# A block inverse that joins four 32-row blocks per product instead of two, in a two-block transformer kernel on one Trainium2 core

## The chip, the core and the metric

The kernel runs on one core of one Trainium2 chip. The engines named below are TensorE (PE, with PEld for its weight loads), VectorE (DVE), ScalarE (ACT), GpSimd (POOL) and SyncE (SP), which here only issues transfers, in the order of its own queue. The metric is the device time of one execution in microseconds (us); lower is better.

## The reference, cut to what matters

Two blocks run one after the other over 1024 tokens of width 1024. The first is the one that matters: a projection `z = h @ w_in`, two branches that read it, their gated sum, and a mixture of experts. One branch is latent attention (`mla_branch`). The other is a recurrence of 8 heads of 64 channels in two directions:

```
    def step(state, inp):
        r_t, w_t, k_t, v_t, a_t, b_t = inp
        sa = jnp.einsum('bhvk,bhk->bhv', state, a_t)
        state = (state * w_t[:, :, None, :] + sa[..., None] * b_t[:, :, None, :]
                 + v_t[..., None] * k_t[:, :, None, :])
        return state, jnp.einsum('bhvk,bhk->bhv', state, r_t)
...
    w_logit = w0.astype(f32) + jnp.einsum('bsdr,drc->bsdc', jnp.tanh(wd), w_up.astype(f32))
...
    a = jax.nn.sigmoid(a0.astype(f32) + jnp.einsum('bsdr,drc->bsdc', ad, a_up.astype(f32)))
```

The second block (windowed attention, a gated linear recurrence, two more mixtures of experts) is not touched.

## The kernel before, in words

The first stage, `branches`, holds everything the change touches. `phase_a` computes z^T in 37 column tiles (`z_tile`: 48 products of 128x512 each) and, between tiles, starts the recurrence. Four head pairs (two heads on 128 partitions) go through four steps:

- `prep(p, d, g)`, for each direction d and each half g of the tokens (so four times per pair): two low-rank products (L579, with the operand `lora_up`) give the decay and the a gate; then mostly VectorE work, two sets of 64-token Gram products (`gram`, L551), and transfers to scratch memory. One result is L, a strictly triangular 64x64 matrix for each chunk of 64 tokens.
- `inverse(p)`: (I - L)^-1 of all 64 matrices of a pair. First the 32x32 diagonal blocks by substitution on VectorE, one block per partition (L653, L655). The result goes to scratch memory E (L656, L658) and comes back as tiles `xn` and `xt`. Then, for each of four units (g, d), the products that fill the off-diagonal block: eight products of 128x128 by 32 columns with L (tile `bd`, L671), a copy to a block diagonal tile (L674 on VectorE, L672 on ScalarE), eight more (L676), a copy on GpSimd and an addition on VectorE (L678, L679), and the transfer to `rw` (`put`, L489). The units share two pairs of tiles and one tile for L, so a unit's loads wait for an earlier unit's products.
- `rwkv_chain(p)`: 16 chunks one after the other, each four sets of small products (L732) with copies between.
- `finish(p, g)`: norm, bonus and gate.

`pair(j)` runs prep four times for pair j, with the inverse and the chain of pair j - 1 behind the first. Latent attention (`mla`) comes last in the program; its inputs z are loaded (L792, L794) once the tiles of `phase_a` are free, then come keys and values (L827, L838), and scores, transposes and values (`S`, L889, L904). After both, `branch_out` takes the results (the products `br`).

The program is written in that order, but a scheduler of the framework, with its own estimates of durations, lays down the order of each engine's instructions. At run time every engine, and SP's queue, follows its order strictly. A pool's buffer that is taken again makes its first writer wait for its last reader.

A float32 product appears in the profile as two records, so eight products are 16 records.

Of the kernel before, what the change touches and what calls it, by code (L numbers as in the profile page):

```python
# [7 lines left out]
F32 = mybir.dt.float32  # L8
# [13 lines left out]

ALPHA = float(np.float32(4.0 ** 0.25))
# [4 lines left out]
# ---------------------------------------------------------------- host layout  # L28

def _cols(w, idx):  # L30
    """[K, M] -> [len(idx)//128, 128, (K//128)*128]: tile, k-partition, (k-block, column)."""
    K = w.shape[0]
    t = w[:, idx].reshape(K // 128, 128, len(idx) // 128, 128)
    return np.ascontiguousarray(t.transpose(2, 1, 0, 3).reshape(len(idx) // 128, 128, K))


def _fvec(v):
    """[n*128] -> [128, n]: feature on the partition."""
    return v.reshape(-1, 128).T


def _chunks(w):
    """[..., K, N] -> [..., N/512 * K/512, 128, 2048]: chunks of 4 k-blocks by 512 columns, k fastest."""
    K, N = w.shape[-2:]
    n = w.ndim - 2
    w = w.reshape(*w.shape[:-2], K // 512, 4, 128, N // 512, 512)
    o = list(range(n)) + [n + x for x in (3, 0, 2, 1, 4)]
    return np.ascontiguousarray(w.transpose(o)).reshape(*w.shape[:n], -1, 128, 2048)


def _constants():
    """Constants of the branches, and those of the whole program."""
# [37 lines left out]
def _vectors(i):  # L90
# [9 lines left out]
    perm = np.concatenate([np.arange(1536, 1920), *[  # L100
# [13 lines left out]
def arrays(i):  # L114
# [8 lines left out]
    order = list(range(1536, 1920))  # L123
# [27 lines left out]
    a["a_up"] = np.ascontiguousarray(i["a_up"][0].reshape(128, 512))  # L151
# [39 lines left out]
# ---------------------------------------------------------------- device program  # L191

class Prog:
# [3 lines left out]
    def consts(self, pool, temp):  # L197
        """pool: for the whole program; temp: for the branches."""
# [17 lines left out]
    def keep(self, keep, dram):  # L216
        """Scratch memory, and the small tiles that several phases use."""
# [37 lines left out]
    def slots(self, table, n, base):  # L255
        """What marks the rows in table [128, 8, n, 6]: the row of its block plus base, the block and zero."""
# [5 lines left out]
    def thirds(self, table, x):  # L262
        """x in three bfloat16 parts that add up to it exactly, to table[..., 3:6]; x is overwritten."""
# [7 lines left out]
    def iota8(self, pool):  # L271
        """The slots (from 1), each eight times."""
# [4 lines left out]
    def onehot(self, out, iota8, pm):  # L277
        """out [128, 128, 8]: 1 at the slot pm (from 1) of each row and row block, 0 elsewhere."""
        return self.nc.vector.tensor_tensor(out, iota8, pm[:, None, :].to_broadcast([128, 128, 8]), op=OP.is_equal)

    def mm3(self, ps, lh, ll, rh, rl, first, last):
        """One K block of a float32 product from operands split into float32r parts."""
# [5 lines left out]
    def order(self, later, first):  # L288
        """`later` is issued behind `first` on their engine: one accumulation at a time in a bank."""
# [3 lines left out]
    def rsqrt(self, pool, out, v, n):  # L293
        """out = v ** -0.5 by Newton steps; out, v: [128, n]."""
# [16 lines left out]
    def rsqrt1(self, pool, out, v):  # L311
        """The same for one column where ScalarE has its square root at hand."""
# [9 lines left out]
def s1(P, hpool, wpool, psum):  # L322
    """Reads x, normalises it and leaves its transpose, split, in hT (hi, lo)."""
# [18 lines left out]
def z_tile(P, spool, psum, hT, m, use):  # L342
    """z^T rows of column tile m of w_in; use(s, ps): the PSUM tile of the tokens s."""
# [15 lines left out]
def phase_a(P, zpool, spool, psum, hT, after=lambda j: None):  # L359
    """z^T = (h @ w_in)^T tile by tile; what later phases need goes to scratch memory."""  # L360
# [81 lines left out]
class Rwkv:  # L442
    """The RWKV branch: a head pair (two heads on 128 partitions) and half of the tokens at a time."""
# [13 lines left out]
    def own(self, dram, pool, psw):  # L457
        """Memory for prep alone."""
        self.pp, self.psw, self.bd, self.n = pool, psw, [], 0
        self.inv = [tuple(pool.tile([128, NH, CH], F32, name=f"x{n}{i}", bufs=1) for n in "nt") for i in range(2)]  # L460
        for a in self.inv:
            for t in a:
                self.P.nc.gpsimd.memset(t, 0.0)
        self.L = [dram.tile([4, 128, NH, CH], F32, name=f"rL{i}") for i in range(2)]
        self.E = [dram.tile([128, 2, 32, 32], F32, name=f"rE{i}") for i in range(2)]
        for b in range(4):
# [9 lines left out]
    def t(self, name, tag="t"):  # L476
        n = {"t": 9, "u": 2, "l": 2}[tag]
# [14 lines left out]
    def stats(self, src, scale, u=None):  # L492
        """[128 (h, ch), 512] -> sums over ch per (token, head): [128 t, 8 = (block, h)] times scale."""
# [7 lines left out]
    def spread(self, st, u=None):  # L501
        """[128 t, 8 = (block, h)] -> [128 (h, ch), 512] in PSUM."""
# [8 lines left out]
    def keys(self, p, g):  # L511
        """Normalised kk of head pair p, negated, to scratch memory."""
# [12 lines left out]
    def flip(self, p, d, g, m, x):  # L525
        """x [128 (h, ch), 512 tokens], transposed per head, to part m of the scratch memory."""
# [10 lines left out]
    def diag(self, i, f):  # L537
        """Block diagonal buffer i, written by f(destination, rows) for each head."""
# [6 lines left out]
    def gram(self, lb, AR, da, mask, dr):  # L545
        """lb^T [A | R] of every chunk (partition: the index of lb), under causal masks."""
# [14 lines left out]
    def prep(self, p, d, g):  # L561
        """Chunks 8 g to 8 g + 7 of head pair p in direction d: all that needs no running state, to memory."""
# [5 lines left out]
        ds = slice(64 * d, 64 * d + 64)  # L568
# [7 lines left out]
        for dst, x, act, b in ((sg, 0, P.twd, self.hb[:, n * d + p:n * d + p + 1]),  # L576
                               (ta, 1, P.ad, self.hb[:, n * (2 + d) + p:n * (2 + d) + p + 1])):
            pm = self.ps(0)
            nc.tensor.matmul(pm, up[ds, x], act[ds, ts], start=True, stop=True)  # L579
            nc.scalar.activation(rv(dst), pm, AF.Tanh, bias=b, scale=0.5)  # L580
# [51 lines left out]
    def inverse(self, p):  # L632
        """(I - L)^-1 of every chunk of head pair p: 32 x 32 diagonal blocks by substitution, one block per
        partition (half, direction, h, block, chunk), then the products that join two blocks."""
# [24 lines left out]
        for u in units:  # L659
            self.n += 1  # L660
            Xn, XT = self.inv[self.n % 2]
            LB = self.bd[2]
            for h in range(2):
                s = slice(64 * h, 64 * h + 64)
                nc.sync.dma_start(LB[s, :, s], L[u, s])
            for x, t in ((0, Xn), (1, XT)):
                for h, b in part:
                    nc.sync.dma_start(t[rows(h, b), :, 32 * b:32 * b + 32], E[at(u, h, b), x].rearrange("c i j -> i c j"))
            ps = self.ps(0).rearrange("p (x c t) -> p x c t", x=2, t=32)
            for c in range(NH):  # L670
                nc.tensor.matmul(ps[:, 0, c], LB[:, c], Xn[:, c, 0:32], start=True, stop=True)  # L671
            for h, copy in ((0, nc.vector.tensor_copy), (1, lambda o, i: nc.scalar.activation(o, i, AF.Copy))):  # L672
                s = slice(64 * h, 64 * h + 64)
                copy(self.bd[3][s, :, 64 * h:64 * h + 32], ps[s, 0])  # L674
            for c in range(NH):
                nc.tensor.matmul(ps[:, 1, c], self.bd[3][:, c], XT[:, c, 32:64], start=True, stop=True)  # L676
            out = self.t3("rXT", "u")
            nc.gpsimd.tensor_copy(out[:, :, 0:32], XT[:, :, 0:32])  # L678
            nc.vector.tensor_add(out[:, :, 32:64], ps[:, 1], XT[:, :, 32:64])  # L679
            self.put(p, u % 2, u // 2, 8, out)  # L680

    def finish(self, p, g, u=None):
        """Group norm, bonus and gate of head pair p; half of o_rwkv^T of the pair."""
# [33 lines left out]
def rwkv_chain(P, pool, psum, p):  # L717
    """The running states of head pair p in both directions over the chunks; leaves y^T in scratch memory."""
# [5 lines left out]
    def mm(ps, terms):  # L724
        # one accumulation group per bank: only its first product clears the bank
# [1309 lines left out]
```

## Time and profile before

| What | Value |
|---|---|
| Median of 3 runs | 4299.33 us (4295.06 to 4307.67) |
| Span of the profiled execution | 4303.5 us |
| TensorE busy over the span | 3854.9 us (90%) |
| VectorE busy | 2887.8 us (67%) |
| ScalarE busy | 2145.3 us (50%) |
| GpSimd busy | 418.9 us (10%) |
| Mean granted TensorE clock | 0.930 of full speed |

The runs' times are of the whole execution, and the profiled span lies inside their spread, 4.2 us above their median. Busy time counts an instruction from its start to its modelled end; the granted clock has two levels, 1.2 and 2.4 GHz, and a mean between 0.5 and 1 tells how a stretch was divided between them.

### The profile page before, as it was taken

To read this page: it belongs to the slowest core of one execution; us is meant where nothing else is said; L and a number is where in the kernel's file an instruction comes from. 1 tells how busy PE (TensorE), PEld (TensorE's weight loads), DVE (VectorE), ACT (ScalarE), POOL (GpSimd) and SP (SyncE) were. 2 spreads that over 40 slices of the span, in tenths; PEclk is the share of its full clock that TensorE was granted. 3 is DMA by queue.
4 is the path that set the end of the run, shared out by engine and by line. 5 is a ranking of instruction groups with operands and counts; after the bars stand their busy time and mean duration, and the time that the engine had idled before them with its cause. 6 is when DMAs were issued, how large, how long until landed. Compare 5 with 4: busy or idle time off the path is not lost. (4 is left out here: it accounts for less than half of the span.)

```text
span 4303.5 us, 57981 instructions
## 1 busy us (share of the span) xinstructions
PE 3854.9 (90%) x22154; PEld 3100.3 (72%) x22154; DVE 2887.8 (67%) x4690; ACT 2145.3 (50%) x2829; POOL 418.9 (10%) x328
## 2 busy tenths in 40 slices
PE   7999988898998897999799969999969986999994
PEld 6877766776876676665679857787748875788773
DVE  4556375858557546654446758888876776788887
ACT  4322223333243224555335536777756852677774
POOL 0000000000010003333000001111010000111101
PEclk9999988988899898999899979999979997999997
DMA  3455665453435557997332359999941155899994
GB/s 106 140 169 148 182 196 161 120 153 92 150 107 173 212 193 269 317 304 227 120 132 82 131 205 338 370 376 384 373 158 69 69 202 207 304 359 377 384 373 168
DMA packets 362342, 925.00 MB, mean 215 GB/s; under 512 B 147600, under 2 KB 205712, under 8 KB 290128
## 3 DMA queue, kind: packets, MB, share of 16 engines
q1 hardware_dynamic: 343632, 870.93, 56.4%
q0 software_dynamic: 18432, 50.36, 4.7%
q8 instruction: 175, 2.87, 0.3%
q14 instruction: 103, 0.84, 0.1%
HBM read 770.68 MB, written 167.25 MB: 218 GB/s over the span
## 5 line engine op out<-in xcount | busy, mean ns | idle before, releaser
L253 DVE TENSOR_TENSOR wlo<-wraw,whi 128x2048 fp32r<-128x2048 f32 x498 | 1134.2, 2289 | 307.1 <-ACT whi L253 303.8
L253 ACT ACTIVATE whi<-wraw 128x2048 fp32r<-128x2048 f32 x498 | 955.0, 1919 | 378.3 <-PE g L286 254.0
L285 PE MATMUL g<-wlo,xth 128*128 128x512 f32 x1280 | 510.0, 398 | 6.7 <-DVE wlo L253 6.7
L284 PE MATMUL g<-whi,xth 128*128 128x512 f32 x1280 | 513.7, 402 | 2.3 <-ACT xth L253 1.6
L286 PE MATMUL g<-whi,xtl 128*128 128x512 f32 x1280 | 508.4, 397 | 7.7 <-DVE xtl L253 7.3
L286 PEld LDWEIGHTS g<-whi,xtl 128*128 128x128 f32 x1280 | 243.5, 190 | 63.7 <-DVE xtl L253 12.7
L285 PEld LDWEIGHTS g<-wlo,xth 128*128 128x128 f32 x1280 | 244.0, 191 | 61.4 <-DVE wlo L253 9.1
L284 PEld LDWEIGHTS g<-whi,xth 128*128 128x128 f32 x1280 | 244.4, 191 | 57.3 <-ACT xth L253 3.9
L284 PE MATMUL z<-hT_hi,w_hi 128*128 128x512 f32 x592 | 243.0, 411 | 9.7 <-ACT w_hi L253 6.7
L1635 POOL DMA_INDIRECT e_xg<-xm,e_ix x32 | 75.5, 2359 | 1719.5 <-DVE e_ix L1633 956.6
L285 PE MATMUL z<-hT_lo,w_hi 128*128 128x512 f32 x592 | 242.0, 409 | 0.0
L286 PE MATMUL z<-hT_hi,w_lo 128*128 128x512 f32 x592 | 241.0, 408 | 0.0
L285 PE MATMUL g<-wlo,e_hh 128*128 128x512 f32 x512 | 202.4, 398 | 15.5 <-DVE wlo L253 15.5
L284 PE MATMUL g<-whi,e_hh 128*128 128x512 f32 x512 | 204.3, 400 | 8.2 <-ACT e_hh L253 8.0
L286 PE MATMUL g<-whi,e_hl 128*128 128x512 f32 x512 | 196.5, 391 | 0.2
L904 PE MATMUL po<-V,pts 128*128 128x64 f32 x1024 | 142.5, 285 | 6.3 <-DVE tab L856 4.9
L284 PEld LDWEIGHTS z<-hT_hi,w_hi 128*128 128x128 f32 x592 | 115.2, 195 | 41.5 <-ACT w_hi L253 7.4
L904 PEld LDWEIGHTS po<-V,pts 128*128 128x128 f32 x1024 | 135.4, 204 | 12.1 <-DVE tab L856 5.2
L755 POOL TENSOR_SCALAR SW<-S,wc 128x64 f32<-128x64 f32 x120 | 65.5, 563 | 785.0 <-DVE S L773 701.3
L285 PEld LDWEIGHTS z<-hT_lo,w_hi 128*128 128x128 f32 x592 | 115.0, 194 | 30.4 <-issue 4.5
L286 PEld LDWEIGHTS z<-hT_hi,w_lo 128*128 128x128 f32 x592 | 114.4, 193 | 30.0 <-issue 3.8
L1235 PE MATMUL g<-wraw,m_hT 128*128 128x512 f32 x256 | 120.3, 610 | 13.1 <-ACT m_y L1236 8.1
(531 smaller groups left out, 8308.7 us busy)
## 6 DMA issues: line engine op xcount, KB each, us to landing
wraw<-in_w_gu SPq DMA_DIRECT2D x256, 1024.0 KB
wraw<-in_w_dn SPq DMA_DIRECT2D x128, 1024.0 KB
wraw<-in_w SPq DMA_DIRECT2D x96, 1024.0 KB
rwt<-rw SPq DMA_DIRECT2D x32, 1152.0 KB
w_raw<-in_w_in SPq DMA_DIRECT2D x37, 512.0 KB
rw<-flip SPq DMA_DIRECT2D x96, 128.0 KB
rw<-rAR SPq DMA_DIRECT2D x16, 512.0 KB
gt<-z_out SPq DMA_DIRECT2D x16, 512.0 KB
```

The costliest lines, as they stand in the source:

```text
L253: return self.nc.scalar.activation(hi, src, AF.Copy), self.nc.vector.tensor_sub(lo, src, hi.bitcast(F32))
L284: t.matmul(ps, lh, rh, start=first, stop=False)
L285: t.matmul(ps, lh, rl, start=False, stop=False)
L286: t.matmul(ps, ll, rh, start=False, stop=last)
L755: nc.gpsimd.tensor_scalar(SW[:, d], S[:, d], P.wc[:, c, 4 * d + p:4 * d + p + 1], None, op0=OP.mult)
L904: i = nc.tensor.matmul(po[:, q], pt[:, k], V[:, 4 * q + k, 64 * par:64 * par + 64], start=(k == 0), stop=(k == 3))
L1235: nc.tensor.matmul(ps, ht[:, k], w[:, k, n], start=(k == 0), stop=(k == 1))
L1635: nc.gpsimd.indirect_dma_start(out=xg, out_offset=None, in_=self.x, in_offset=bass.IndirectOffsetOnAxis(ap=ix[:, :1], axis=0))
```

## The change

Two things change in the stage `branches`. First, the inverse: the four 32-row blocks of one half of the tokens (two directions, two heads) stand on the four quarters of the 128 partitions, so that one product with a tile of four diagonal 32x32 blocks serves both directions. The loop runs over the two halves g instead of the four units. All loads of a pair are asked for ahead of the products, into tiles that the halves don't share, and the copies out of PSUM are of 32 rows, half of them on VectorE and half on ScalarE; the last ones go straight into the tile that is put to memory. Second, the weights and columns of the low-rank part are permuted so that the two products of one prep read different halves of the 128 rows, and both products are written ahead of both activations. To make room, the scratch of the software-made transfers (those of GpSimd) is halved from the framework's default of 16384 bytes.

```
+LORA = np.r_[1536:1664, 1728:1792, 1664:1728, 1792:1920]
...
-    a["a_up"] = np.ascontiguousarray(i["a_up"][0].reshape(128, 512))
+    a["a_up"] = np.ascontiguousarray(i["a_up"][0][::-1].reshape(128, 512))
...
-        self.inv = [tuple(pool.tile([128, NH, CH], F32, name=f"x{n}{i}", bufs=1) for n in "nt") for i in range(2)]
+        self.inv = [pool.tile([128, NH, CH], F32, name=f"xt{i}", bufs=1) for i in range(4)]
...
-        for b in range(4):
+        for b in range(5):
             t = pool.tile([128, NH, 128], F32, name=f"bd{b}", bufs=1)
...
-        ds = slice(64 * d, 64 * d + 64)
+        rows = [slice(64 * x, 64 * x + 64) for x in (d, 1 - d)]
...
-        for dst, x, act, b in ((sg, 0, P.twd, self.hb[:, n * d + p:n * d + p + 1]),
-                               (ta, 1, P.ad, self.hb[:, n * (2 + d) + p:n * (2 + d) + p + 1])):
-            pm = self.ps(0)
-            nc.tensor.matmul(pm, up[ds, x], act[ds, ts], start=True, stop=True)
-            nc.scalar.activation(rv(dst), pm, AF.Tanh, bias=b, scale=0.5)
+        pm = [self.ps(0) for x in range(2)]
+        for x, act in enumerate((P.twd, P.ad)):
+            nc.tensor.matmul(pm[x], up[rows[x], x], act[rows[x], ts], start=True, stop=True)
+        for x, dst in enumerate((sg, ta)):
+            o = n * (2 * x + d) + p
+            nc.scalar.activation(rv(dst), pm[x], AF.Tanh, bias=self.hb[:, o:o + 1], scale=0.5)
...
-        for u in units:
-            self.n += 1
-            Xn, XT = self.inv[self.n % 2]
-            LB = self.bd[2]
-            for h in range(2):
-                s = slice(64 * h, 64 * h + 64)
-                nc.sync.dma_start(LB[s, :, s], L[u, s])
-            for x, t in ((0, Xn), (1, XT)):
+        X1, X2 = (pool.tile([128, 2 * NH, 32], F32, name=x, bufs=1) for x in ("rX1", "rX2"))
+        quad = [(d, h, slice(64 * d + 32 * h, 64 * d + 32 * h + 32)) for d in range(2) for h in range(2)]
+        cs = [slice(NH * g, NH * g + NH) for g in range(2)]
+        for g in range(2):
+            for d, h, q in quad:
+                u = 2 * g + d
+                nc.sync.dma_start(self.bd[2 + g][q, :, q], L[u, 64 * h:64 * h + 32, :, 32:64])
+                nc.sync.dma_start(X1[q, cs[g]], E[at(u, h, 0), 0].rearrange("c i j -> i c j"))
+                nc.sync.dma_start(X2[q, cs[g]], E[at(u, h, 1), 1].rearrange("c i j -> i c j"))
+            for d in range(2):
                 for h, b in part:
-                    nc.sync.dma_start(t[rows(h, b), :, 32 * b:32 * b + 32], E[at(u, h, b), x].rearrange("c i j -> i c j"))
+                    nc.sync.dma_start(self.inv[2 * g + d][rows(h, b), :, 32 * b:32 * b + 32],
+                                      E[at(2 * g + d, h, b), 1].rearrange("c i j -> i c j"))
+        copies = (nc.vector.tensor_copy, lambda o, i: nc.scalar.activation(o, i, AF.Copy))
+        for g in range(2):
             ps = self.ps(0).rearrange("p (x c t) -> p x c t", x=2, t=32)
             for c in range(NH):
-                nc.tensor.matmul(ps[:, 0, c], LB[:, c], Xn[:, c, 0:32], start=True, stop=True)
-            for h, copy in ((0, nc.vector.tensor_copy), (1, lambda o, i: nc.scalar.activation(o, i, AF.Copy))):
-                s = slice(64 * h, 64 * h + 64)
-                copy(self.bd[3][s, :, 64 * h:64 * h + 32], ps[s, 0])
+                nc.tensor.matmul(ps[:, 0, c], self.bd[2 + g][:, c], X1[:, NH * g + c], start=True, stop=True)
+            for d, h, q in quad:
+                copies[h](self.bd[4][q, :, q], ps[q, 0])
             for c in range(NH):
-                nc.tensor.matmul(ps[:, 1, c], self.bd[3][:, c], XT[:, c, 32:64], start=True, stop=True)
-            out = self.t3("rXT", "u")
-            nc.gpsimd.tensor_copy(out[:, :, 0:32], XT[:, :, 0:32])
-            nc.vector.tensor_add(out[:, :, 32:64], ps[:, 1], XT[:, :, 32:64])
-            self.put(p, u % 2, u // 2, 8, out)
+                nc.tensor.matmul(ps[:, 1, c], self.bd[4][:, c], X2[:, NH * g + c], start=True, stop=True)
+            for d, h, q in quad:
+                copies[h](self.inv[2 * g + d][64 * h:64 * h + 32, :, 32:64], ps[q, 1])
+            for d in range(2):
+                self.put(p, d, g, 8, self.inv[2 * g + d])
...
-    nc = bacc.Bacc("TRN2", target_bir_lowering=False, num_devices=1)
+    nc = bacc.Bacc("TRN2", target_bir_lowering=False, num_devices=1, dynamic_dma_scratch_size=8192)
```

The scheduler lays down new orders for the stage. On TensorE, the inverse of the second head pair begins like this before the change; the products of one unit are `xn` with `bd` and, some rows on, `xt` with `bd` (each row x8), and latent attention's keys and values (`pj`) stand between.

```order
L671 MATMUL pw<-xn_189,bd_203 128x32 x8
L732 MATMUL pc<-p_2718,rwt 64x64 x4
L827 MATMUL pj<-zk,wk 128x512 x2
...
L838 MATMUL pj<-wv,zk 128x128
L676 MATMUL pw<-xt_190,bd_205 128x32 x8
L838 MATMUL pj<-wv,zk 128x128 x2
L732 MATMUL pc<-p_2768,rwt 64x64 x4
L671 MATMUL pw<-xn_187,bd_203 128x32 x8
```

At the same place after the change, the whole inverse is four such rows (`rX` with `bd`), and the next prep's two low-rank products stand between them:

```order
L680 MATMUL pw<-rX_3921,bd_203 128x32 x8
L740 MATMUL pc<-S,rwt 64x64 x4
L740 MATMUL pc<-rwt 64x64 x4
L740 MATMUL pc<-p_2684,rwt 64x64 x4
L684 MATMUL pw<-rX_3922,bd_207 128x32 x8
...
L680 MATMUL pw<-rX_3921,bd_205 128x32 x8
L580 MATMUL pw<-twd,lora_up 128x512
...
L684 MATMUL pw<-rX_3922,bd_207 128x32 x8
L580 MATMUL pw<-ad,lora_up 128x512
```

The eight groups have become four, attention's keys have moved behind them, and the two low-rank products have three rows between them (two of the chain and the last group). In all 16 preps of the changed order there are rows between the two (2 to 22); in the order before they are neighbours in one prep of 16.

In SP's queue, after the last tile of `phase_a`, attention's inputs stood ahead of the second pair's inverse; its store of E comes as `rE` further down:

```order
L485 DMA v<-zr_102 128x512
L792 DMA zk<-zm_109 128x1024
L792 DMA zk<-zm_110 128x1024
L794 DMA zq<-zm_106 128x1024
L593 DMA kd_140<-t_3749 128x512
L794 DMA zq<-zm_107 128x1024
L794 DMA zq<-zm_108 128x1024
```

After the change the store of E stands behind `v`, ahead of `kd`, and attention's inputs come behind the inverse's loads and the first two of its four puts:

```order
L674 DMA xt_189<-rE_198 32x8x32 x4
L674 DMA xt_190<-rE_198 32x8x32 x4
L490 DMA rw_129<-xt_187 128x4x128
L490 DMA rw_129<-xt_188 128x4x128
L649 DMA rLd<-rL_195 8x32x32 x4
L669 DMA bd_203<-rL_195 32x8x32 x2
L800 DMA zk<-zm_109 128x1024
L800 DMA zk<-zm_110 128x1024
L802 DMA zq<-zm_106 128x1024
```

So the loads of `zk` and `zq` have moved past the puts, which wait for products.

## Rows read from the trace of the kernel before

**Rows 1.** Windows: busy us (instructions) by engine, granted clock, DMA share, GB/s.

```profile
core 0: us, PE busy (x) PEld busy (x) DVE busy (x) ACT busy (x) POOL busy (x), PEclk, DMA share, GB/s
600.00:640.00 40.00, 25.35 (x261) 20.53 (x256) 29.66 (x55) 11.42 (x28) 6.73 (x9) 0.79 0.85 261
640.00:690.00 50.00, 42.12 (x252) 34.63 (x252) 13.21 (x28) 10.75 (x24) 3.39 (x7) 0.55 0.43 111
690.00:850.00 160.00, 140.18 (x1280) 113.49 (x1279) 137.43 (x337) 66.18 (x164) 9.78 (x18) 0.93 0.51 147
850.00:905.00 55.00, 47.83 (x368) 40.68 (x366) 16.83 (x39) 12.11 (x31) 4.35 (x10) 0.73 0.46 114
905.00:1080.00 175.00, 155.06 (x1377) 124.06 (x1378) 136.73 (x328) 66.88 (x167) 12.35 (x20) 0.89 0.45 131
1080.00:1135.00 55.00, 53.43 (x376) 46.61 (x373) 15.39 (x46) 10.16 (x27) 3.30 (x8) 0.66 0.46 121
1135.00:1360.00 225.00, 221.90 (x2585) 179.28 (x2583) 145.09 (x415) 96.04 (x265) 22.19 (x49) 0.99 0.37 124
1360.00:1430.00 70.00, 46.39 (x273) 31.74 (x273) 43.29 (x94) 19.24 (x30) 2.01 (x4) 0.77 0.68 238
```

**Rows 2.** Timeline of PE, end of the stage: start, us, line, product, idle before.

```profile
1364.28 0.66 PE L943 MATMUL pj<-cst,O 128*128 128x128 f32 x4 [0.69 <-ACT ot L945]
...
1377.61 0.64 PE L732 MATMUL pc<-rwt,U 64*64 64x64 f32 x8
...
1392.00 1.41 PE L284 MATMUL br<-oh,whi 128*128 128x512 f32 x1
```

**Rows 3.** Groups by line: busy us, mean ns of one, idle before and its causes.

```profile
L671 PE MATMUL pw<-xn,bd 128*128 128x32 f32 x256 | 44.6, 333 | 10.0 <-DMA bd<-rL 8.4 <-DMA xt<-rE 1.6
L676 PE MATMUL pw<-xt,bd 128*128 128x32 f32 x256 | 40.8, 322 | 8.7 <-ACT bd L672 6.3 <-DMA xt<-rE 2.4
L579 PE MATMUL pw<-twd,lora_up 64*128 64x512 f32 x32 | 20.8, 734 | 0.0
L579 PE MATMUL pw<-ad,lora_up 64*128 64x512 f32 x32 | 18.8, 669 | 0.9 <-DVE nkk L522 0.9
```

**Rows 4.** Timeline of PE, three groups of the third inverse's products.

```profile
864.11 1.97 PE L676 MATMUL pw<-xt,bd 128*128 128x32 f32 x16
...
880.25 1.03 PE L671 MATMUL pw<-xn,bd 128*128 128x32 f32 x4 [6.86 <-DMA bd<-rL]
...
889.05 3.62 PE L676 MATMUL pw<-xt,bd 128*128 128x32 f32 x16
```

**Rows 5.** Timeline of SP's queue during the second inverse: start, us of issuing, transfers.

```profile
602.95 0.90 SPq L792 DMA_DIRECT2D zk<-zm  x2
...
605.54 0.32 SPq L593 DMA_DIRECT2D kd<-t  x1
...
619.33 0.32 SPq L658 DMA_DIRECT2D rE<-rLd  x1
...
639.46 1.93 SPq L668 DMA_DIRECT2D xt<-rE  x4
...
663.01 0.38 SPq L489 DMA_DIRECT2D rw<-rXT  x1
...
684.13 0.38 SPq L489 DMA_DIRECT2D rw<-rXT  x1
685.64 0.33 SPq L572 DMA_DIRECT2D lora_up<-in_w_up  x1
```

**Rows 6.** Timeline of PE, end of the projection and attention's first keys.

```profile
593.46 0.40 PE L286 MATMUL z<-hT_hi,w_lo 128*128 128x512 f32 x1
...
622.86 1.98 PE L827 MATMUL pj<-zk,wk 128*128 128x512 f32 x4 [0.27 <-ACT ot L803]
```

**Rows 7.** Groups by line: the copies between the products, 300 to 1140 us.

```profile
L674 DVE COPY bd<-pw 64x256 f32<-64x256 f32 x16 | 6.7, 416 | 33.6 <-PE pw L671 33.6
L672 ACT ACTIVATE bd<-pw 64x256 f32<-64x256 f32 x16 | 6.0, 378 | 48.1 <-DVE bd L674 48.1
```

**Rows 8.** The page's costliest groups: a software-made transfer.

```profile
L1635 POOL DMA_INDIRECT e_xg<-xm,e_ix x32 | 75.5, 2359 | 1719.5 <-DVE e_ix L1633 956.6 <-PE tr L1057 724.5 <-DVE e_oh L279 25.1
```

More of the change, by code (lines that the diff above doesn't have):

```diff
@@ L98, in add @@
         cols.append(a)
-    perm = np.concatenate([np.arange(1536, 1920), *[
+    perm = np.concatenate([LORA, *[
         np.concatenate([np.arange(128 * p, 128 * p + 128) + 512 * s for s in range(3)]) for p in range(4)]])
@@ L122, in arrays @@
     a["x"] = np.ascontiguousarray(i["x"].reshape(8, 128, D))
-    order = list(range(1536, 1920))
+    order = list(LORA)
     for p in range(4):
@@ L457, in own @@
     def own(self, dram, pool, psw):
-        self.pp, self.psw, self.bd, self.n = pool, psw, [], 0
-        self.inv = [tuple(pool.tile([128, NH, CH], F32, name=f"x{n}{i}", bufs=1) for n in "nt") for i in range(2)]
-        for a in self.inv:
-            for t in a:
-                self.P.nc.gpsimd.memset(t, 0.0)
+        self.pp, self.psw, self.bd = pool, psw, []
+        self.inv = [pool.tile([128, NH, CH], F32, name=f"xt{i}", bufs=1) for i in range(4)]
+        for t in self.inv:
+            self.P.nc.gpsimd.memset(t, 0.0)
         self.L = [dram.tile([4, 128, NH, CH], F32, name=f"rL{i}") for i in range(2)]
         self.E = [dram.tile([128, 2, 32, 32], F32, name=f"rE{i}") for i in range(2)]
-        for b in range(4):
+        for b in range(5):
             t = pool.tile([128, NH, 128], F32, name=f"bd{b}", bufs=1)
@@ L476, in t @@
     def t(self, name, tag="t"):
-        n = {"t": 9, "u": 2, "l": 2}[tag]
+        n = {"t": 9, "l": 2}[tag]
         return (self.big if tag == "t" else self.pp).tile([128, HT], F32, name=name, tag=tag, bufs=n)
```

## The prediction, made before the changed kernel ran

> **What bounds the kernel now.** I first looked in the page's forty slices for the place of the changed lines: they lie in the first third of the span. The chain of waits reaches back from the end only into the expert stages, so it says nothing here; the stage has to be read from windows. Those show a rhythm [rows 1]. In three long stretches VectorE is full (137.43 of 160 us, then 136.73 of 175): preps and substitutions. Between them lie the joins of the inverses (640 to 690, 850 to 905, 1080 to 1135), where VectorE has almost nothing to do (13 to 17 us) and TensorE's granted clock is 0.55 to 0.73. From 1135 to 1360 TensorE is busy 221.90 of 225 us at a clock of 0.99. The end of the stage shows what decides: attention's last products are at 1364, the last chain's at 1378, `branch_out` starts at 1392 [rows 2]. So attention and the recurrence end together and TensorE is full in the last 225 us: what it is spared earlier should arrive as time, since the work that fills it is only moved forward.
>
> The joins are long because they wait: from the second store of E at 619.33 to the last put at 684.13 the second inverse takes 65 us, and the next prep's weights (`lora_up`, 685.64) stand behind that put in SP's queue [rows 5]. VectorE therefore starts its next full stretch only then.
>
> **The change part by part.**
>
> *Half of the products.* 512 records of L671 and L676 are busy 44.6 + 40.8 = 85.4 us [rows 3]. Eight groups of 16 records per pair become four of the same shape, so 42.7 us go. The price of a group is 1.97 us at the high clock and 3.62 at the low one [rows 4]: 16 groups fewer are worth 31.5 us if all ran at 2.4 GHz and 57.9 if all at 1.2. I take 42.7, the mix that the trace shows.
>
> *Waits at these products.* TensorE sat idle 10.0 + 8.7 = 18.7 us in front of them, for `bd` and `xt` loads that a shared tile held back and for the copy between the two sets [rows 3]. The loads now come ahead; the copy stays. Bounds 0 and -18.7; I take half, -9.4.
>
> *The clock in the joins.* After the 6.86 us wait at 880 the next groups run at the low level (3.62 us against 1.97) [rows 4]. The three joins hold 42.12 + 47.83 + 53.43 = 143.4 us of TensorE work at clocks of 0.55, 0.73 and 0.66 [rows 1]; about three quarters of the 85.4 are products of the inverse, which leaves some 79 us of other work at about 0.65. At the 0.93 of the stretch in between that would be 55 us, so the bounds are 0 and -24. The shorter joins still have copies and puts to wait for: I take a third, -8.
>
> *The copies.* Per pair VectorE has eight small instructions before and eight after, ScalarE eight instead of four, GpSimd four fewer; ScalarE is idle most of the stage (10 to 12 us busy in each join [rows 1]), so that is where the extra ones hide. What stands on the path is the row of copies between two sets: now 0.42 + 0.38 us, one after the other (L672 waited 48.1 us for L674 in all) [rows 7]. Four 32-row copies have as many elements per partition, so I price them alike: at most 1.6 us in place of 0.8, twice per half instead of once per unit plus an addition. That is about 1.5 us more per pair if nothing overlaps, 6 in all, 0 if the two engines run side by side; I take +3.
>
> *The loads* are 40 per pair before and after, at about 0.48 us of issue each (1.93 for four) [rows 5], so SP's issue time stays. The transfers are no larger.
>
> *Attention's inputs move.* This is the one thing in the new order that speaks against the change. Before, the loads of `zk` were issued at 602.95 [rows 5] and the first keys came at 622.86, after the projection's last product at 593.46 [rows 6]. Now they stand behind 32 loads and two puts of the second inverse. The store of E now precedes the `kd` store, which was at 605.54 [rows 5], and everything is a little earlier because the first inverse gives back some 8 us; say E is stored at 600. Then 32 loads (15.4 us), about ten other transfers (6 us) and six small loads put `zk` at 625 or so, some 20 us later. In 600 to 640 TensorE was busy 25.35 of 40 us [rows 1] even with attention's first products in it; I count half of the 20 us as new idle time, +9 to +10: I take +9. Bounds: 0 if the chain and the prep fill it, +20 if nothing does. What is queued behind the waiting puts is attention alone; the next prep's weights follow only three places behind its last load and come far earlier than before.
>
> *The low-rank products.* Both are written ahead of both activations, on different row halves. They are busy 20.8 + 18.8 = 39.6 us [rows 3]. TensorE's queue keeps rows of 128x512, 64x64 or 128x128 products between the two in every prep of the new order, so neither has its partner beside it: 0. The bounds are 0 and -19.8. Against that: the Trainium skill, TensorEngine Tiling, section Tiling Modes (Key Properties), says that different tiles of the array can load and multiply in parallel. By that rule two neighbouring half-row products would take the time of one, and the sum would be 19.8 us lower; no run here shows such a pair yet, and the order gives the rule nothing to act on.
>
> *The halved scratch* concerns GpSimd's transfers, all of them in the expert stages. GpSimd sat idle 1719.5 us in front of the 32 loads of L1635 alone [rows 8], so waiting there is covered: 0. Without that cover each of them would be late by what it waits, and I have no row for that.
>
> Sum: -42.7 - 9.4 - 8 + 3 + 9 = -48.1 us, from 4303.5 to 4255.4. The profiled span is 4.2 us above the median of the runs, 4299.33; against that median the same sum gives 4251.
>
> **The rivals.**
>
> *A. The freed time turns into waits (small gain).* VectorE's two full stretches stay as they are, and if the recurrence, not TensorE, is what the end waits for, or attention's late start costs its full +20, only part of 42.7 arrives. For it: 86% busy VectorE from 690 to 850. Against it: TensorE at 221.90 of 225 at the end. Price: 31.5 us of products less 20 is -11.5, to about -25 with a few waits gone: 4274 to 4288.
>
> *B. The joins' waits and clock come back whole.* -42.7 - 18.7 - 24 = -85.4: 4214. For it: two rounds instead of four, and no load between them. Against it: copies, puts and SP's order remain.
>
> *C. The low-rank halves overlap after all*, with each other or with neighbouring half-row products of the chain: -48 - 19.8 = -68: 4231. Against it: the order.
>
> *D. Slower: attention waits for the second inverse.* The place is SP's queue at the two puts ahead of `zk`. If the second put went out as late as before (663.01 [rows 5]), attention's inputs would come about 65 us after 602.95; with half to all of that idle on TensorE, +33 to +65 replaces the +9, and the total is -24 to +8. It turns slower if the put comes later than that by 10 us or more, for instance at 680 with nothing to fill TensorE: +82 - 57 = +25, 4324.
>
> *E. The halved scratch holds GpSimd's transfers back*, or the new order in the stage cancels the gain in some other place: within 13 us of before, 4299.
>
> **How the numbers follow.** A measurement of this kernel can tell about 0.3%, 13 us. Chances: my forecast 0.62, A 0.15, B 0.09, C 0.06, D 0.04, E 0.04. The predicted time is 4251. The forecast's own terms, each at its bounds, run from about -70 to -30: 4229 to 4269. For 8 in 10 the range reaches into A and B: 4212 to 4286. Faster by over 0.3%: forecast, B, C and most of A, 0.87. Within: the rest of A, half of E and a little of D, 0.08. Slower: 0.05.
>
> **What would show it right or wrong.** In the changed profile: the two lines of the inverse's products with 128 records each (L680, L684), 40 to 45 us together; the low-rank products about as busy as before, 38 to 41 us. From the second inverse's store of E to its last put about 30 us instead of 65, and the next `lora_up` some 40 to 50 us earlier than 685.64. Attention's first keys later than 622.86 with an idle TensorE ahead of them: 630 to 635. The first `br` product at about 1344 instead of 1392, and everything behind it moved by the same amount. If `br` comes that early and the end does not, a later stage took it back; if the joins are short and `br` is hardly earlier, A holds; if the low-rank lines fall to half, C.

## The result

The changed kernel takes 4226.77 us (median of 4 runs, 4223.6 to 4245.4), the kernel before 4301.41 us in the same session (4295.06 to 4307.67): a ratio of 0.9842, 95% interval 0.9818 to 0.9865 (the two medians alone would give 0.983; one of the four runs, 4245.4, lies 18 us above the other three). The profiled execution of the changed kernel has a span of 4221.8 us, that of before 4303.5.

The windows of the changed kernel, at the places of [rows 1] (same columns):

```profile
core 0: us, PE busy (x) PEld busy (x) DVE busy (x) ACT busy (x) POOL busy (x), PEclk, DMA share, GB/s
600.00:640.00 40.00, 31.16 (x253) 25.25 (x254) 15.61 (x37) 11.60 (x28) 2.12 (x5) 0.62 0.80 221
640.00:690.00 50.00, 39.48 (x329) 29.55 (x328) 37.60 (x76) 21.71 (x48) 3.43 (x6) 0.86 0.70 210
850.00:905.00 55.00, 52.66 (x430) 42.47 (x432) 40.12 (x91) 23.77 (x57) 1.72 (x4) 0.92 0.67 188
1080.00:1135.00 55.00, 54.68 (x726) 43.78 (x724) 33.12 (x90) 25.62 (x76) 6.87 (x16) 1.00 0.32 106
```

Where the joins stood, VectorE is now busy 33 to 40 us instead of 13 to 17, and the clock is 0.86 to 1.00 instead of 0.55 to 0.73: the next preps run there. The groups of the changed lines (compare [rows 3]):

```profile
L684 PE MATMUL pw<-rX,bd 128*128 128x32 f32 x128 | 20.6, 320 | 4.3 <-issue 4.2
L580 PE MATMUL pw<-twd,lora_up 64*128 64x512 f32 x32 | 18.9, 672 | 0.0
L580 PE MATMUL pw<-ad,lora_up 64*128 64x512 f32 x32 | 18.9, 672 | 0.0
L680 PE MATMUL pw<-rX,bd 128*128 128x32 f32 x128 | 16.9, 291 | 5.9 <-DMA rX<-rE 5.9
```

The inverse's products fell from 85.4 to 37.5 us, the waits in front of them from 18.7 to 10.2; the low-rank products stayed (37.8 against 39.6). SP's queue in the second inverse ([rows 5] before):

```profile
589.77 0.32 SPq L661 DMA_DIRECT2D rE<-rLd  x1
622.73 0.95 SPq L490 DMA_DIRECT2D rw<-xt  x2
627.20 1.08 SPq L800 DMA_DIRECT2D zk<-zm  x2
...
635.11 0.33 SPq L574 DMA_DIRECT2D lora_up<-in_w_up  x1
636.33 0.38 SPq L490 DMA_DIRECT2D rw<-xt  x1
```

From the store of E to the last put it takes 46.6 us instead of 65, and the next `lora_up` is 50.5 us earlier. Attention's inputs are 24 us later than before, its first keys 16 us (639.13 against [rows 6]). Then the end of the stage, on PE (compare [rows 2]):

```profile
639.13 3.78 PE L835 MATMUL pj<-zk,wk 128*128 128x512 f32 x4 [0.76 <-ACT ot L811]
...
1278.75 1.12 PE L951 MATMUL pj<-cst,O 128*128 128x128 f32 x4 [0.69 <-ACT ot L953]
...
1283.93 0.40 PE L740 MATMUL pc<-rwt,U 64*64 64x64 f32 x8
...
1298.02 0.80 PE L286 MATMUL br<-oh,whi 128*128 128x512 f32 x1 [7.58 <-ACT whi L255]
```

Attention and the last chain still end together, 86 and 94 us earlier than before, and the first `br` is 94 us earlier. But `branch_out`'s second part, the products `wo`, starts at 1393.53 instead of 1461.15: 67.6 us. To account for these I read windows from the first inverse's second store of E (377.20 before, 376.88 after) to the first `wo`, divided at the chain's end; before first, then after:

```profile
377.00:1376.10 999.10, 913.32 (x7981) 737.11 (x7979) 617.73 (x1529) 336.68 (x819) 75.94 (x142) 0.89 0.49 146
1376.10:1461.10 85.00, 60.39 (x236) 43.41 (x236) 51.22 (x101) 20.89 (x24) 0.00 (x0) 0.80 0.67 243
```

```profile
377.00:1282.20 905.20, 836.82 (x7694) 666.86 (x7692) 602.41 (x1492) 341.50 (x832) 64.60 (x126) 0.93 0.51 154
1282.20:1393.50 111.30, 72.94 (x266) 48.02 (x266) 64.36 (x137) 22.59 (x27) 0.00 (x0) 0.76 0.62 219
```

TensorE's busy time in this stage fell by 64 us (973.7 to 909.8), its idle time by 4 (110.4 to 106.7). Of the 64, 47.9 are the products that went; the other 16 are the same work at a higher clock (0.91 for the whole stretch, 0.89 before). The 16 rest on one profile of each kernel. Two kernels below with nearly the same orders agree (scratch_only 976.1 busy, inverse_only 907.4), but lora_only, profiled in the fastest of its 12 runs, has 948.5 in scratch_only's order. Behind the chain the stage became 26 us longer (111.3 against 85), and this takes back part of the 94: more of `finish` is left there, beside `branch_out` (eight records of its first product, `y` with `cstb`, instead of four), at a clock of 0.76 instead of 0.80. From the first `wo` to the end it is 2842.4 us before and 2828.3 after; over the profiles of all the timed kernels below that stretch, which none of them edits, is 2828 to 2844. So 14 us of the 81.7 between these two spans lie in work that no edit touches, and 67.6 in the stage. The stage scatters too: scratch_only, below, has the order of before up to the chain's end, and reaches it 9.9 us earlier.

### The profile page after: what moved, and what is told of

It is laid out like the page before. It is cut to its first block, busy times and chain, and to the rows that moved or that the text cites. A ratio compares the mean times of both kernels' runs of the same rounds, so it can differ in the third digit from the quotient of the medians.

```text
span 4221.8 us, 57401 instructions
## 1 busy us (share of the span) xinstructions
PE 3787.8 (90%) x21898; PEld 3031.0 (72%) x21898; DVE 2887.3 (68%) x4690; ACT 2153.3 (51%) x2845; POOL 404.0 (10%) x313
## 5 line engine op out<-in xcount | busy, mean ns | idle before, releaser
L288 PE MATMUL g<-whi,e_hl 128*128 128x512 f32 x512 | 196.5, 391 | 0.2
```

The lines of the kernel that those rows point to most:

```text
L288: t.matmul(ps, ll, rh, start=False, stop=last)
```

## The experiments

Two theories stood against each other. Theory 1: what counts is how long the four joins last on the recurrence's path, from E's store to the last put. Theory 2: TensorE's work is the time. "Before" ran beside every set (medians 4298.6 to 4301.4). In order of time:

| Kernel | Median us | Ratio to before, 95% | E's second store to last put, sum of four joins, us |
|---|---|---|---|
| before | 4299 | 1 | 250.3 |
| lora_only | 4289.07 | 0.9973 (0.9960 to 0.9986) | 239.3 |
| scratch_only | 4285.77 | 0.9971 (0.9957 to 0.9984) | 247.7 |
| own_tiles | 4276.50 | 0.9943 (0.9924 to 0.9963) | 224.3 |
| twice | 4256.59 | 0.9903 (0.9880 to 0.9926) | 211.9 |
| merged | 4245.57 | 0.9884 (0.9865 to 0.9904) | |
| two_queues | 4236.35 | 0.9850 (0.9833 to 0.9867) | 171.9 |
| pool_queue | 4234.45 | 0.9851 (0.9828 to 0.9875) | 166.9 |
| spare | 4227.78 | 0.9834 (0.9809 to 0.9859) | 170.6 |
| inverse_only | 4227.64 | 0.9827 (0.9810 to 0.9844) | 156.1 |
| after | 4226.77 | 0.9842 (0.9818 to 0.9865) | 152.9 |
| adjacent | 4219.07 | 0.9817 (0.9795 to 0.9838) | 150.8 |
| trip | 4218.44 | 0.9819 (0.9802 to 0.9837) | |

**The low-rank part put back (inverse_only).**

> The changed kernel with the low-rank part put back (old row halves, each product directly ahead of its activation); the joins and the halved scratch stay as changed. Theory 1 (the gain is the time that the four joins take on the recurrence's path, from the second store of E to the last put): all of the gain is here, 4220 to 4240 us. Theory 2 (the gain is TensorE's work removed, 48 us of products plus some waits): the same. Rival C (the low-rank halves bring up to 19.8 us): 4245 us or more.

```
-        pm = [self.ps(0) for x in range(2)]
-        for x, act in enumerate((P.twd, P.ad)):
-            nc.tensor.matmul(pm[x], up[rows[x], x], act[rows[x], ts], start=True, stop=True)
...
+            pm = self.ps(0)
+            nc.tensor.matmul(pm, up[ds, x], act[ds, ts], start=True, stop=True)
```

4227.64 us: as the changed kernel. In the two traces the order of instructions is the same on every engine, so nothing else changed with the edit: all of the gain is there without the low-rank part.

**The low-rank part alone (lora_only), and the scratch alone (scratch_only).**

> The kernel before with only the low-rank part of the change and the halved scratch; the inverse is as it was. Theories 1 and 2: as before, within 6 us of 4301. Rival C: 4281 us. If the halved scratch holds GpSimd's transfers back: above 4310 us.

> The kernel before with only the scratch for GpSimd's transfers halved. If the 0.27% of the run of the low-rank part came from the scratch: 4289 us. Theory 1: it came from the order of transfers in the last joins, which this kernel leaves as it was: within 6 us of before, 4293 to 4305 us.

```
-    nc = bacc.Bacc("TRN2", target_bir_lowering=False, num_devices=1)
+    nc = bacc.Bacc("TRN2", target_bir_lowering=False, num_devices=1, dynamic_dma_scratch_size=8192)
```

Both gain 0.3%, and by the same amount, so the low-rank part is worth nothing that these runs can tell beside the scratch, and the scratch alone is worth some 13 us (0.16 to 0.43%). Theory 1's number for the scratch, within 6 us of before, was wrong, and lora_only's 4289 is neither the 4301 of both theories nor rival C's 4281. The profiles suggest the place. In the kernel before, the loads of attention's result for `branch_out` (`oraw`) stand in SP's queue behind the chain's last store of y:

```profile
1382.56 0.80 SPq L780 DMA_DIRECT2D yd<-Y  x2
...
1385.79 1.37 SPq L996 DMA_DIRECT2D oraw<-om  x3
```

With the scratch halved the scheduler's order, the same up to this place, is another one from here on; the loads come ahead of that store (lora_only has the same order in SP's queue):

```profile
1362.14 1.38 SPq L996 DMA_DIRECT2D oraw<-om  x3
...
1370.95 0.79 SPq L780 DMA_DIRECT2D yd<-Y  x2
```

From the chain's end to the first `wo`, scratch_only first, then lora_only:

```profile
1366.20:1441.40 75.20, 61.15 (x236) 42.48 (x237) 50.37 (x101) 22.53 (x27) 0.00 (x0) 0.81 0.70 250
1356.50:1431.00 74.50, 60.12 (x237) 41.49 (x238) 50.32 (x101) 22.54 (x27) 0.00 (x0) 0.82 0.70 254
```

Both are 10 us shorter than the 85 of before, and TensorE is idle 14 us there instead of 25. That the loads' place does this is argued; no run moves the loads alone. In the changed kernel `oraw` stands behind the store again (1287.33 behind 1285.19), so this gain can't simply be taken as a share of its 75 us; no run has the changed inverse without the halving.

**Loads ahead, products as before (own_tiles).**

> The kernel before with all 512 product records of the four inverses and their four rounds per pair, but with tiles of their own for the units' loads, so that (but for two small loads of the last unit) no load waits for a product or a put; the copies behind the second products go in place on two engines, as in the changed kernel; the scratch is halved. Theory 1 (what the joins take on the recurrence's path sets the gain): the joins lose the waits for shared tiles, and a third to two thirds of the gain of 75 us comes although no product is removed: 4250 to 4276 us. Theory 2 (TensorE's removed work is the gain): only waits of TensorE can come back, 18.7 us at most and half of it likely: 4280 to 4294 us.

```
-            Xn, XT = self.inv[self.n % 2]
-            LB = self.bd[2]
...
+            Xn, XT = self.inv[u]
+            LB = LBs[u]
```

With full tiles for all four units a pool of the kernel finds 26.6 KB per partition where it needs 32.5 (the run ahead, which has no time for that reason), so here `xn` has 32 columns and the last unit shares a tile for L. The copies behind the second products are those of the changed kernel.

4276.50 us, 9 below scratch_only (the halved scratch is in both). This lies between the ranges of the two theories and decides for neither. The loads ahead bring some 0.3%; four rounds of products with their copies remain. But the new order also put attention's inputs behind the second inverse (632.83 against 606.68 in scratch_only), so what the loads ahead are worth by themselves may be more.

**The products twice in the joins (twice), and as many outside them (spare).**

> The changed kernel with every product of the joins issued twice over, so that the joins hold 512 records again, on their path. Both theories: the 37.5 us of these lines are busy a second time, and most of it arrives: 4252 to 4266 us. With the next run it is a pair: the same work on the path and off it.

```
-            for c in range(NH):
+            for c in [*range(NH), *range(NH)]:
                 nc.tensor.matmul(ps[:, 0, c], self.bd[2 + g][:, c], X1[:, NH * g + c], start=True, stop=True)
...
```

> The changed kernel with 256 more records of the joins' shape, 128x32, but in the preparations ahead of the products of gram, where VectorE is what is full; their results are overwritten. Theory 1: TensorE has slack there, so much less than the 37 us of work arrives: 4227 to 4242 us. Theory 2: work is work: 4252 to 4266 us, as with the products doubled in the joins.

```
+            for c in range(2):
+                nc.tensor.matmul(ps[:, 128 * c:128 * c + 32], lb[:, 4 * g + c], AR[:, 4 * g + c, 0:32], start=True, stop=True)
```

The added records are the same in number and shape. Against the changed kernel twice costs 29.8 us in the median, spare 1.0; their intervals are clear of one another. The groups, of twice (both lines, in all) and of spare (the added ones):

```profile
L684 PE MATMUL pw<-rX,bd 128*128 128x32 f32 x256 | 51.0, 372 | 0.9 <-issue 0.9
L680 PE MATMUL pw<-rX,bd 128*128 128x32 f32 x256 | 42.4, 330 | 0.0
```

```profile
L552 PE MATMUL pw<-rAR,bd 128*128 128x32 f32 x256 | 40.1, 282 | 5.2 <-DVE bd L613 4.8
```

In the joins the additional work is busy 93.4 - 37.5 = 55.9 us, in the preparations 40.1. From the start to the first `wo`, the changed kernel, spare and twice:

```profile
0.00:1393.50 1393.50, 1260.21 (x9548) 993.64 (x9548) 891.00 (x2137) 490.89 (x1062) 72.29 (x141) 0.93 0.49 154
0.00:1388.70 1388.70, 1279.90 (x9804) 1015.58 (x9804) 888.47 (x2137) 492.04 (x1062) 72.51 (x141) 0.95 0.50 154
0.00:1415.60 1415.60, 1312.64 (x9805) 1048.26 (x9806) 889.35 (x2140) 494.06 (x1065) 79.51 (x141) 0.92 0.49 151
```

In spare TensorE is busy only 20 us longer for 40 us of new work, because it ran at a higher clock (0.95 against 0.93), and its idle time fell from 133 to 109. In twice it is busy 52 us longer and idle 30 us less, and the first `wo` is 22 us later. Theory 2 falls here: the same records cost nothing that can be measured in the preparations and some 30 us in the joins. The scheduler laid down a new order for each of the two, which is part of what is compared.

**A longer way for E (trip).**

> The changed kernel in which E makes one more trip in each inverse: stored, loaded back and stored again before its transpose is made. No engine has more work; two transfers' time is added between the substitution and the joins. From the rows of before a store and the load behind it lie about 2 us apart, so some 4 to 6 us per inverse. Theory 1: three quarters of 16 to 24 us arrive, as the runs so far show for the joins' lengths: 4238 to 4246 us. Theory 2: as the changed kernel, 4222 to 4232 us.

```
         nc.sync.dma_start(E[:, 0], X)
+        nc.sync.dma_start(X, E[:, 0])
+        nc.sync.dma_start(E[:, 0], X)
```

From the first store of E to the last put the four joins now last 187.8 us instead of 159.7, and the last put is 37 us later. Yet the kernel takes 4218.44 us, 8 less than the changed one and below both numbers. The edit moved something else with it: in the new order attention's inputs go out ahead of the second inverse (583.81 instead of 627.20), and its first keys come at

```profile
600.08 1.88 PE L837 MATMUL pj<-zk,wk 128*128 128x512 f32 x4
```

against 639.13. So attention is done before the chain, and `branch_out` starts beside it (`br` at 1282.92; the chain's last products are at 1305):

```profile
1269.94 1.38 SPq L1006 DMA_DIRECT2D oraw<-om  x3
...
1284.13 1.56 SPq L790 DMA_DIRECT2D yd<-Y  x2
1306.58 0.80 SPq L790 DMA_DIRECT2D yd<-Y  x2
```

TensorE is busy 906.52 us of the stage, as in the changed kernel, and idle 83 instead of 107. Two things changed at once, so trip alone judges nothing; with adjacent, below, it does.

**The loads on another queue (two_queues, pool_queue), and fewer, larger ones (merged).**

> The changed kernel with 16 of the 40 loads of a join (those of the transposed blocks) issued from ScalarE's queue in place of SP's. No product, copy or transfer is removed. Theory 1: SP issues 16 loads of about 0.49 us less in each join, 7.8 us of which some lie beside other waits; 10 to 25 us below the changed kernel, 4202 to 4217 us. Theory 2: as the changed kernel, 4222 to 4232 us.

> The changed kernel with 16 of a join's 40 loads issued from GpSimd's queue, on which next to nothing stands in the joins, where ScalarE's held copies of the chain up. Theory 1: SP's issue of 16 loads goes from the joins, 7.8 us each, but a transfer made by GpSimd may take longer to issue and to land: if the joins get shorter by 2 to 6 us each, 4205 to 4222 us; if they get longer, the time goes up with them. Theory 2: as the changed kernel, 4222 to 4232 us, whatever the joins do.

> The changed kernel with E laid out in memory so that the 16 loads of X1 and X2 of an inverse become 4 of four times the size, and its two stores four. Products, copies and bytes are the same; SP issues ten instructions less in each join, about 4.9 us. Theory 1: the joins get shorter by 2 to 5 us each, 4215 to 4224 us, unless the large loads land later than the small ones did. Theory 2: as the changed kernel.

```
-                    nc.sync.dma_start(self.inv[2 * g + d][rows(h, b), :, 32 * b:32 * b + 32],
+                    nc.scalar.dma_start(self.inv[2 * g + d][rows(h, b), :, 32 * b:32 * b + 32],
...
-                nc.sync.dma_start(X1[q, cs[g]], E[at(u, h, 0), 0].rearrange("c i j -> i c j"))
...
+                nc.sync.dma_start(t[:, cs[g]], E[x, g, 8 * x:8 * x + 8].rearrange("c q (i j) -> (q i) c j", j=32))
```

(The first pair is two_queues; pool_queue has `gpsimd` there. The second is merged.) All three made the joins longer (merged 196.5 us from the first store, against 159.7), and none became faster, against my numbers for two_queues and merged. Merged's median is 19 us higher, and its interval only touches the changed kernel's; the medians of two_queues and pool_queue are 10 and 8 us higher, but their intervals overlap the changed kernel's for the most part, so they can't be told from it. On ScalarE the loads stand between copies that the chain waits for (ACTq are the loads):

```profile
1020.10 2.87 ACTq L674 DMA_DIRECT2D xt<-rE  x4
1023.07 0.27 ACT L748 ACTIVATE p<-pc 64x128 f32<-64x128 f32 x1 [4.16 <-DMA rX<-rE]
1023.10 2.39 ACTq L674 DMA_DIRECT2D xt<-rE  x5
1028.21 0.27 ACT L748 ACTIVATE U<-pc 64x128 f32<-64x128 f32 x1 [4.87 <-DVE U L747]
```

In merged three of the four large loads of the last join went out only between 1030.68 and 1038.04, and the first product waited 6.12 us for one of them (`rX`); the small ones of the changed kernel take 0.45 us each there. In all inverses these waits are 24.9 us (L683) instead of 5.9. Fewer instructions on SP were no gain.

In merged and pool_queue too the new order put attention's inputs ahead of the second inverse; merged first, then pool_queue:

```profile
598.34 1.46 SPq L803 DMA_DIRECT2D zk<-zm  x2
...
610.23 1.23 SPq L661 DMA_DIRECT2D rE<-rX  x2
```

```profile
591.62 0.42 SPq L800 DMA_DIRECT2D zk<-zm  x1
...
605.26 0.33 SPq L659 DMA_DIRECT2D rE<-rX  x1
```

Their first keys come at 614.42 and 614.95, some 24 us before the changed kernel's, and neither is faster. So an early attention by itself does not make a kernel faster than the changed one.

**The low-rank halves side by side (pairs, adjacent).**

> The changed kernel with 48 more low-rank products in each of two preparations of the first head pair, next to one another on TensorE: in the first alternating between the two halves of the rows, in the second 24 on one half and then 24 on the other. The results are overwritten. Rival C's rule (two halves work side by side): the alternating ones start half as far apart as those on one half. If not: equally far apart in both.

> The changed kernel with the two low-rank products of every preparation directly behind one another on TensorE (a product of two columns ahead of them takes both places in PSUM first). In the run with repeated pairs two records on different halves started in 0.43 us, two on one half in 0.86; so the second product of a pair (two records) should start some 0.1 us behind the first instead of 0.86, which spares TensorE up to 16 times 0.86 = 13.8 us. If such work counts in full: 4213 us. As in the run with 256 more records in the preparations, where TensorE's work moved nothing: 4222 to 4232 us.

```
+        i = nc.tensor.matmul(pm[1][:, 0:2], up[rows[1], 1], P.ad[rows[1], 0:2], start=True, stop=True)
         for x, act in enumerate((P.twd, P.ad)):
-            nc.tensor.matmul(pm[x], up[rows[x], x], act[rows[x], ts], start=True, stop=True)
+            j = nc.tensor.matmul(pm[x], up[rows[x], x], act[rows[x], ts], start=True, stop=True)
+            P.order(j, i)
+            i = j
```

Pairs is read for its starts alone, not for its time. The alternating records (L582, L583) start 0.11 and 0.32 us apart, two in 0.43; those on one half (L586) take 19.58 us for 45, 0.435 each:

```profile
188.34 0.59 PE L583 MATMUL pw<-ad,lora_up 64*128 64x512 f32 x1
188.45 0.59 PE L582 MATMUL pw<-twd,lora_up 64*128 64x512 f32 x1
188.77 0.59 PE L583 MATMUL pw<-ad,lora_up 64*128 64x512 f32 x1
188.88 0.59 PE L582 MATMUL pw<-twd,lora_up 64*128 64x512 f32 x1
...
234.10 19.58 PE L586 MATMUL pw<-twd,lora_up 64*128 64x512 f32 x45
```

So two halves do work side by side. The Trainium skill, TensorEngine Tiling, section Tiling Modes (Key Properties), says so, and this trace agrees. In adjacent, one pair of the stage:

```profile
865.98 0.69 PE L581 MATMUL pw<-twd,lora_up 64*128 64x512 f32 x1
865.99 0.69 PE L581 MATMUL pw<-ad,lora_up 64*128 64x512 f32 x1
866.51 0.59 PE L581 MATMUL pw<-twd,lora_up 64*128 64x512 f32 x1
866.52 0.59 PE L581 MATMUL pw<-ad,lora_up 64*128 64x512 f32 x1
867.04 0.66 PE L900 MATMUL pt<-cst,p 128*128 128x128 f32 x4
```

Both products are through in 1.06 us, the time of one of them alone in the changed kernel. The low-rank products, with the added ones of two columns, are busy 25.5 us in adjacent instead of 37.8. 4219.07 us is 8 less than the changed kernel, between my two numbers, and the two intervals overlap. Here too the order put attention's inputs ahead of the second inverse (first keys at 593.53, `br` at 1276.88), so whether the 8 us come from the pairs, from attention or from chance stays open. Against trip it tells this: both have attention early, trip's joins are longer by 27 us (187.8 against 160.6 from the first store) and its low-rank products are spread as before in all but one preparation, and the times are equal. The last put goes out at 1051.38 in adjacent and at 1061.77 in trip, 27 and 37 us later than in the changed kernel (1024.46), and neither is slower. With that, theory 1 in its plain form falls: in these orders the joins' length is not what the end waits for.

## Why the prediction came out as it did

The likeliest time was 4251 us, the measured one is 4226.77: the sign holds, and of the mechanism the halved products; the size was too small, -48 against -68 in the stage that the change touches. Read along the medians of the experiments, the gain comes in four steps: the scratch 13 us (scratch_only), the loads ahead 9 (own_tiles), two rounds for four 20 (twice), and half of the records 30 (the changed kernel). Each step also has an order of its own, so these are no exact shares. They still show where the sum went short by 24 us: two steps worth 33 us together had nothing in it, and the halved records brought about 30 instead of 42.7. That the result lies well inside the range is in part luck, since these misses have opposite signs.

- *Half of the products*, -42.7: measured -47.9, since those that remain run at 291 and 320 ns instead of 333 and 322. How much of this arrives is shown by twice: put back on the path, 55.9 us of busy time cost 29.8 us, about half; TensorE is idle 30 us less.
- *Waits at these products*, -9.4: 18.7 became 10.2, so -8.5. With the scratch and all 512 records, in own_tiles, the kernel is 9 us below scratch_only, with intervals of some 8 and 6 us to either side.
- *The clock in the joins*, -8: too small. TensorE's other work of the stage was busy 16 us less in the two profiles, at 0.91 from 377 to the first `wo` instead of 0.89. I had let the clock rise a little inside the joins; but with the joins 153 us long instead of 250, what ran there at a low clock now runs beside preps, at 0.86 to 1.00.
- *The copies*, +3: the four copies of a set do go one after the other, VectorE and ScalarE in turn, ScalarE idle 15.5 and 19.9 us behind VectorE's. But two rounds with them are still cheaper than four: twice has as many records as own_tiles and two rounds instead of four, and is 20 us faster. My sum had no term for the rounds themselves.
- *Attention's inputs*, +9: they came as late as forecast (`zk` at 627.20; the keys at 639 even later than 630 to 635). The idle TensorE that I named as its sign did not appear: in 600 to 640 it was busy 31.16 us instead of 25.35, though at a clock of 0.62 instead of 0.79. No run shows the price by itself: in trip and adjacent, with the inputs 43 and 56 us earlier, the median is 8 us lower; in merged and pool_queue, with them 29 and 36 us earlier, it is 19 and 8 us higher. The size of this term stays open.
- *The low-rank products*, 0: right for the order as it is, shown by inverse_only; rival C is true of the chip and had no pair to act on.
- *The halved scratch*, 0: wrong. I named GpSimd's idle time as its cover and overlooked that the halving changes the scheduler's order; alone it is worth 0.3%.
- *"Three long stretches" of full VectorE*: the rows show two, as the rivals' part says; no term rests on the third.
- *"The first `br` at about 1344, and everything behind it moved by the same amount"*: it failed twice. `br` is at 1298, and 26 of its 94 us are given back before `wo`, where more of `finish` is left beside `branch_out`. That is a little of rival A, behind a good deal of rival B.

Terms summed as measured in the stage: -47.9 products, -16 clock, -4 idle time in all (forecast: -42.7 products, -8 clock, -9.4 + 3 + 9 = +2.6 for waits, copies and inputs): -68.

What stays open: how much of the gain is the scratch's in the changed kernel, how far the four steps depend on the order that each got, and what attention's early start is worth by itself. Trip and adjacent are below the changed kernel in the median, by less than the intervals can tell.

## What to carry to other kernels

Price work by where it stands: the same 256 records cost 30 us inside a serial stretch with a low clock, and nothing that could be measured in a stretch where another engine is full. Read a stage as TensorE's busy and idle time up to the same product in both kernels, and follow the gain to the point where another branch joins, since it can be given back there. And any edit, even to a memory size far from the stage, can change a scheduler's order: measure it alone where that is possible, and compare the orders before giving an edit the credit.

## What the runs showed of the hardware

- A kernel with more work on TensorE can run at a higher granted clock: with 256 additional records the clock from the start to the first `wo` went from 0.93 to 0.95, and over the whole execution it is 0.940 to 0.945 in the five runs of spare against 0.933 to 0.940 in the nine of the changed kernel and inverse_only. Trip, which adds no such work, has 0.940 to 0.944, so whether the work or the new order raised it is not shown.
- Two float32 products of 64 rows on different halves, neighbours on TensorE, take the time of one (1.06 us for both), while each record's own duration stays at 0.59 to 0.69 us: the durations do not show the overlap, the starts do.
- A group of lines busy 37.5 us, doubled in its place, became 93.4, not 75: mean times rose from 291 and 320 to 330 and 372 ns. From a join's first product to its last the clock was 0.56 to 0.67 in twice, 0.59 to 1.00 in the changed kernel.
